# FFN groups of two blocks: side pieces handed out beside the first down products instead of the last up block's

## The chip, the cores and the metric

The kernel runs on one core of one Trainium2 chip. The metric is the device time of one launch, in microseconds. The engines are TensorE (PE in the profile, with its weight loads as PEld), VectorE (DVE), ScalarE (ACT), GpSimd (POOL) and SyncE (SP), which here only issues DMAs.

## What is computed

One inference step of a hybrid decoder layer (DEPTH 1) over 1024 prompt tokens and 64 sample tokens (8 sequences of 8), 1088 in all, model width 1024, FFN width 2752:

```
h = x + 1/2 * postnorm(SwiGLU_1(prenorm(x)))
u = prenorm(h); z = u @ w_in            # forgetting attention (8 heads x 64) and gated linear attention (4 heads)
h = h + postnorm(concat(A_out, B_out) @ w_out)
y = h + 1/2 * postnorm(SwiGLU_2(prenorm(h)))

def swiglu(x, w_gu, w_down):
    gate, up = jnp.split(x @ w_gu, 2, axis=-1)
    return (jax.nn.silu(gate) * up) @ w_down
```

All norms are RMS norms. Everything is float32; the kernel gets float32 accuracy from TensorE by splitting each operand into a high and a low part and adding three products (high x high, high x low, low x high).

## The kernel before

**Layout.** Activations lie transposed: the model width on 128 partitions in 8 slices, tokens along the free dimension. The tokens are worked in two parts, 0 to 511 (one chunk of 512 columns) and 512 to 1087 (chunks of 256 and 320 columns). Each FFN runs once for each part, so there are four passes: `f1a` and `f1b` for FFN 1, `f2` and `f3` for FFN 2.

**Blocks and groups.** The hidden width is cut into 22 blocks, block 0 being a half-wide tail. Blocks are worked in groups of two or four. For an ordinary group each block has a gate job (`job_gate`, line 674) and an up job (`job_up`, line 683): 8 slices of the model width times three products for each chunk, accumulated in one PSUM bank. The up block's evacuation (`up`, line 567) multiplies gate and up on DVE (line 539 or 540), casts the high part on ACT and subtracts it on DVE (both recorded at line 213, in `split`). When all blocks of the group are through, four down jobs (`job_down`, line 783) add the group's part of the output, two output slices at a time; within each, the products of all blocks but the last come first (`downs`, line 607), and DVE adds the result to `y` (line 646) and so frees the bank. Many groups take another path (`job_first`, `job_seven`, `job_last`) that computes gate and up in a different way; they do not go through `job_up`.

**Where two-block groups go through `job_up`.** `GROUPS` ends in [18, 19] and [20, 21], `GROUPS1` in [20, 21]. By the plans at lines 2034, 2168 and 2174 this is so in five places: block 21 in `f1a`; blocks 19 and 21 in `f1b`; blocks 19 and 21 in `f2`.

**Side pieces.** Norms, evacuations of the projection and the preparation of other stages are written as generators. `beside` (line 266) puts one into a list, `quick` or `side`. Each group of products ends in `tick(us)` (line 243) with an estimate of its own time, operations x columns x `COL` (line 44). `tick` first writes out pending evacuations (`flush`), moves the planned time `now` on, and calls `step_side` (line 253), which advances every generator of `quick` and the first of `side` whose due time has come by one piece. A piece yields the planned time until its next one; without a number that is `STEP`, 2 us. After that `tick` hands out pieces of the background list `bg` at a rate of their own.

**The norm** (line 381) is the generator that matters around the change. Its pieces are: squares and their sum (`square`, line 321; ACT, DVE, POOL) with the product `ncol` on PE that sums over partitions (line 346) and a power on POOL; a diagonal (line 366); the product `nrows` that spreads the factor over rows (line 373) with the first two slices of the scaling (line 414 with the residual added at 415, or line 439 with the splitting at 441 and 442); then two slices each. A norm with `post` and `pre` does all of this twice, with 6 planned us in between (`DREDUCE`). `need(key)` (line 376) hands out pieces without regard to their due time until the norm named is through. Around the places in question:

- before [18, 19] of `f1b`, `next2` (line 2028) puts up two norms of 256 tokens each for part one; the projection's first job needs both (line 2071);
- before [20, 21] of `f2`, the output projection puts up norms of 256 and 320 tokens for part two; the first job of `f3` needs them (line 2180).

**Order on an engine.** What is written out is given its order on each engine by the program that builds the kernel, which may place an instruction ahead of earlier ones that wait. Two things hold it: `keep_in_program_order`, and the pin in `step_side` (line 258), which puts a piece's instructions behind the last noted one of their engine while `pin` is set. `next1` (line 2014) clears it and `later_norm` (line 487) sets it.

Of the kernel before, what the change touches and what calls it, by code (L numbers as in the profile page):

```python
# [71 lines left out]
class Sums:  # L72


    def __init__(self, gate, up, f, first=None):
        self.gate, self.up, self.f = gate, up, f
        self.i = 0 if first is None else first.count
        self.first = first or self
        self.first.count = self.i + 1
# [98 lines left out]
class Step:  # L178
    def __init__(self, ctx, tc, A, O):
        self.ctx, self.tc, self.nc, self.A, self.O = ctx, tc, tc.nc, A, O  # L180
        nc = self.nc
        self.const = ctx.enter_context(tc.tile_pool(name="const", bufs=1))
        self.dram = ctx.enter_context(tc.tile_pool(name="dram", bufs=1, space=DRAM))
        self.n = 0
        self.side, self.quick, self.bg, self.pend = [], [], [], []
        self.ncw, self.ssb, self.xb = NCW, 3, 2
        self.ready = set()
        self.kept, self.later = False, []
        self.last, self.pin = {}, True
        self.calm, self.haste = False, 0.0  # L190
        self.plain, self.begin = None, lambda feed: None
        self.ups = 0
        self.held = False
        self.rate = self.due = self.now = 0.0
        self.near = None
        self.banks = dict(col=("col", 1), col2=("col", 1), rows=("rows", 1))
        cp = self.const
        self.ident = cp.tile([P, P], F32, name="ident")
        make_identity(nc, self.ident)
        self.ones = cp.tile([P, P], F32, name="ones")  # L200
        nc.vector.memset(self.ones, 1.0)
        self.mhalf = cp.tile([P, 4], F32, name="mhalf")
        nc.vector.memset(self.mhalf, -0.5)
        self.gain = cp.tile([P, 6, KB], F32, name="gain")
# [38 lines left out]
    def tick(self, us):  # L243

        self.flush()
        self.now += us
        self.step_side()
        self.due += us * self.rate
        while self.due >= 1:
            self.due -= 1  # L250
            self.piece()
# [265 lines left out]
    def ffn(self, w_gu, w_dn, f):  # L517
# [4 lines left out]
        gu = lambda i: [w_gu[i]]  # L522
# [14 lines left out]
        def times(out, t, u):  # L537
            if f.tanh:
                return nc.vector.scalar_tensor_tensor(out=out, in0=t, scalar=0.5, in1=u, op0=ALU.mult, op1=ALU.mult)
            return nc.vector.tensor_tensor(out=out, in0=u, in1=t, op=ALU.mult)  # L540

        def rooted(out, src, rb):
            self.mark = self.note(nc.vector.tensor_tensor(out=out, in0=src, in1=rb, op=ALU.mult)).ins

        def rows(o):
            return None if f.rb is None else f.rb[:, o]

        def release(c0, n, fn):

            held = [] if f.rb is None else [f.hold[c] for c in f.hold if c0 <= c < c0 + n and f.hold[c] is not None]  # L550
            held[-1].append(fn) if held else self.soon(fn)
# [15 lines left out]
        def up(hb, w, c0, n):  # L567
            o = slice(c0 - f.b0, c0 - f.b0 + n)
            ps = self.gemm(w, c0, n)
            hh, hl = hid[hb]  # L570
            t, rb = sgs[hb][:, o], rows(o)

            def evac():
                self.mark = self.note(times(t, t, ps)).ins
                if rb is not None:
                    rooted(t, t, rb)
                    self.ups += 1
                self.split(hh[:, o], hl[:, o], t, True)
            release(c0, n, evac)
# [80 lines left out]
        def job_first(g, ws):  # L660
            make(g)
            for hb in g:
                sg(hb)
            for i, (c0, n) in enumerate(f.firsts):
                f.first(i)
                if f.room and len(g) == 2 and i == len(f.firsts) - 1 and not f.early:
                    self.beside(sevens(), True)
                tail(ws[0], c0, n)
                if i == len(f.firsts) - 1:
                    self.feed.free(1, NW)  # L670
                gate(g[1], ws[1], c0, n)
                up(g[1], ws[2], c0, n)

        def job_gate(g, hb, w, chunks):
            if hb == g[0]:
                make(g)
            if f.room and hb == 2 and HB_TAIL in g and f.rb is None:
                self.beside(sevens(), True)
            sg(hb)
            for c in chunks:  # L680
                gate(hb, w, *c)

        def job_up(hb, w, chunks):
            for c in chunks:
                up(hb, w, *c)

        def seven(z, w, half, b, done):

            hi, lo = w
            xh, xl = f.operands[b]  # L690
            n = f.n // 2
            z.turn = (z.turn + 1) % 2
            ps = self.mm(n) if z.turn or self.nmm > 3 else self.other(n)
            for k in range(KB // 2):
                s = slice((half * KB // 2 + k) * P, (half * KB // 2 + k + 1) * P)
                ops = [(hi[:, s], xh[:, k]), (hi[:, s], xl[:, k]), (lo[:, s], xh[:, k])]
                for j, (a, x) in enumerate(ops):
                    nc.tensor.matmul(ps, a, x, start=(k == 0 and j == 0), stop=(k == KB // 2 - 1 and j == len(ops) - 1))  # L698
                self.tick(len(ops) * n * COL)

            def evac():
                late = self.later[:1]
                del self.later[:1]
                done(ps)
                for fn in late:
                    fn()
            self.soon(evac)
# [104 lines left out]
        jobs = []  # L812
        for g, chunks, kind in f.plan:
            if kind == "jobs":
                jobs += chunks
                continue
            if kind == "first":
                jobs.append(([gu(0), gu(1), gu(2)], lambda *ws, g=g: job_first(g, ws), 1))
                for hb in g[2:]:
                    jobs.append(([gu(2 * hb - 1)], lambda w, g=g, hb=hb, c=chunks: job_gate(g, hb, w, c), 0))  # L820
                    jobs.append(([gu(2 * hb)], lambda w, hb=hb, c=chunks: job_up(hb, w, c), 0))
            elif kind == "last":
                up4 = [gu(2 * hb - 1 + i) for hb in g for i in range(2)]
                dn = [[w_dn[d2][:, 2 * P * g[0]:2 * P * (g[-1] + 1)] for d2 in d] for d in ((0, 1), (2, 3))]
                reqs = up4[:3] + [(r, f.place(i)) for i, r in enumerate([up4[3]] + dn)]
                jobs.append((reqs, lambda *ws, g=g, c=chunks: job_last(g, ws, c), 0))
                continue
            elif kind == "sevens":
                for hb in g:
                    z, first = Part(), None  # L830
                    for i in range(4):
                        it = Sums(w_gu[2 * hb - 1], w_gu[2 * hb], f, first)
                        first = first or it
                        jobs.append(([it], lambda w, g=g, hb=hb, i=i, z=z: job_seven(g, hb, i, z, w), 0))
            else:
                for hb in g:
                    jobs.append(([gu(2 * hb - 1)], lambda w, g=g, hb=hb, c=chunks: job_gate(g, hb, w, c), 0))
                    jobs.append(([gu(2 * hb)], lambda w, hb=hb, c=chunks: job_up(hb, w, c), 0))
            if g[0] in f.between:
                jobs.append(([], f.between[g[0]], 0))  # L840
            fin = kind == "final"
            cs = [c for c in CH if chunks[0][0] <= c[0] < sum(chunks[-1])] if fin and not f.raw else chunks
            ds = []
            if kind == "sevens":
                ds = list(range(3 - len(cs)))
                jobs.append(([[w_dn[d2][:, 2 * P * g[0]:2 * P * (g[-1] + 1)]] for d2 in ds],
                             lambda *ws, g=g, ds=ds, cs=cs: downs(g, [(d2, w, None, *c, 0, None) for d2, w in zip(ds, ws) for c in cs], False), 0))
            for d2 in range(len(ds), 4):
                jobs.append(([[w_dn[d2][:, 2 * P * g[0]:2 * P * (g[-1] + 1)]]], lambda w, g=g, d2=d2, cs=cs, fin=fin: job_down(g, d2, w, cs, fin), 0))
# [1440 lines left out]
```

## Time and profile before

| | us |
|---|---|
| median of three runs | 2268.49 (2267.0 to 2269.81) |
| the profiled execution, its own time | 2272.61 |
| its span in the profile | 2270.7 |
| granted TensorE clock, mean | 0.997 |

Where the five places lie in the span, from the up block's last products to the end of the group's down products (us from the span's start):

| pass, group | up block | down products |
|---|---|---|
| `f1a`, [20, 21] | 352.35 to 357.8 | to 368.9 |
| `f1b`, [18, 19] | 700.5 to 707.1 | to 723.7 |
| `f1b`, [20, 21] | 743.6 to 750.3 | to 765.4 |
| `f2`, [18, 19] | 1749.5 to 1753.8 (its later part) | to 1765.1 |
| `f2`, [20, 21] | 1836.5 to 1842.0 | to 1856.0 |

How to read the rows: in a timeline a row is start, duration, engine, line of the kernel, operation, output tile and input tiles (names without their numbers), the form of the operands and a count; in brackets stands how long the engine had been idle before it and what released it. In the busy time by stages each row is a stretch of the span. In the groups of instructions, the numbers behind the bar are busy time in us, the mean of one in ns, and the idle time of the engine just before them.

### The profile page before, as it was taken

The numbers are of one execution on the slowest core, as the hardware profiler recorded it, in microseconds if no ns is written. First come the engines' busy times: TensorE is split into PE (matmuls) and PEld (weight loads), VectorE is DVE, ScalarE is ACT, GpSimd is POOL, SyncE is SP. The second block draws the span as 40 slices with busy tenths as digits, with TensorE's granted clock in tenths as the row PEclk, the third lists the DMA queues.
The fourth block names the chain that finished last, engine by engine and source line by source line (L and its number), as shares of the span: only waits on it lengthen the run. The fifth ranks groups of instructions, "written<-read, shape, count | busy, mean of one in ns | idle before, by whom it ended". The sixth has DMA issues, their size and how long they took to land.

```text
span 2270.7 us, 40551 instructions
## 1 busy us (share of the span) xinstructions
PE 2223.8 (98%) x15040; PEld 1984.0 (87%) x15040; DVE 1538.4 (68%) x2678; ACT 1029.0 (45%) x1783; POOL 624.9 (28%) x570
## 2 busy tenths in 40 slices
PE   9999999999999999999999999999999999999998
PEld 8898888999999877899898677777777989999998
DVE  7877886876777885566455333358775688678866
ACT  6544445433344465755344222236555556333432
POOL 2433331442223322011332312311100144234413
PEclk9999999999999999999999999999999999999999
DMA  5333333322234586563656899955554653324324
GB/s 185 122 105 96 98 102 126 102 82 82 93 112 126 166 263 198 176 195 119 202 172 201 297 336 328 316 161 141 165 152 134 199 176 112 99 89 140 103 80 139
DMA packets 203526, 357.25 MB, mean 157 GB/s; under 512 B 27265, under 2 KB 102594, under 8 KB 202946
## 3 DMA queue, kind: packets, MB, share of 16 engines
q1 hardware_dynamic: 187426, 316.36, 44.1%
q0 software_dynamic: 6544, 21.50, 2.7%
q10 hardware_dynamic: 9360, 16.81, 2.2%
q8 instruction: 119, 1.95, 0.4%
q14 instruction: 77, 0.63, 0.1%
HBM read 308.93 MB, written 45.65 MB: 156 GB/s over the span
## 4 chain that ended last, share of the span: by engine, by line
PE 47%; DVE 7%; issue 6%; ACT 3%; DMA 3%; POOL 1%; ACTq 0%; SPq 0%; DVEq 0%; POOLq 0%
PE mm L230 30%; PE mm L698 3%; PE mx L698 3%; DVE wl L213 2%; PE po L1463 2%; PE sp L1201 1%; PE po L1239 1%; PE tp L1447 1%; ACT wh L213 1%; PE pa L1596 1%; DMA wr<-in_wd 1%; DMA wr<-in_wout 1%; PE s L1430 1%; PE s L1429 1%; PE pS L1639 1%
## 5 line engine op out<-in xcount | busy, mean ns | idle before, releaser
L213 DVE TENSOR_TENSOR wl<-wr,wh 128x1024 fp32r<-128x1024 f32 (+1 forms) x251 | 290.1, 1158 | 170.0 <-ACT wh L213 152.0
L230 PE MATMUL mm<-ua,wh 128*128 128x512 f32 (+2 forms) x1264 | 391.9, 393 | 1.1 <-ACT ua L213 0.6
L213 ACT CAST wh<-wr 128x1024 fp32r<-128x1024 f32 (+1 forms) x251 | 245.3, 979 | 304.7 <-PE mm L230 175.3
L230 PE MATMUL mm<-ub,wh 128*128 128x256 f32 (+3 forms) x1760 | 372.4, 306 | 0.9 <-ACT st L968 0.5
L230 PE MATMUL mm<-hl,wh 128*128 128x256 f32 (+2 forms) x1006 | 330.1, 330 | 0.7 <-DVE hl L213 0.6
L230 PE MATMUL mm<-hh,wh 128*128 128x256 f32 (+2 forms) x958 | 320.1, 335 | 10.3 <-DVE y L646 6.3
L230 PE MATMUL mm<-hh,wl 128*128 128x256 f32 (+2 forms) x958 | 315.1, 329 | 2.2 <-DVE wl L213 2.2
L230 PEld LDWEIGHTS mm<-ub,wh 128*128 128x128 f32 (+1 forms) x1760 | 282.5, 189 | 10.7 <-issue 4.6
L230 PEld LDWEIGHTS mm<-ua,wh 128*128 128x128 f32 (+1 forms) x1264 | 225.6, 188 | 55.2 <-issue 14.1
L230 PE MATMUL mm<-ub,wl 128*128 128x256 f32 (+2 forms) x864 | 258.9, 300 | 1.0 <-DVE wl L213 1.0
L698 PE MATMUL mm<-ub,wh 128*128 128x288 f32 (+1 forms) x1328 | 258.3, 290 | 0.0
L230 PE MATMUL mm<-ua,wl 128*128 128x512 f32 (+1 forms) x624 | 239.5, 384 | 0.0
L646 DVE TENSOR_TENSOR y<-y,mm 128x256 f32<-128x256 f32 (+2 forms) x275 | 136.8, 524 | 113.8 <-PE mm L230 111.2
L698 PEld LDWEIGHTS mm<-ub,wh 128*128 128x128 f32 x1328 | 210.8, 189 | 0.0
L230 PEld LDWEIGHTS mm<-hh,wh 128*128 128x128 f32 x958 | 180.7, 189 | 32.2 <-issue 7.7
L230 PEld LDWEIGHTS mm<-hl,wh 128*128 128x128 f32 x1006 | 190.0, 189 | 15.0 <-DVE hl L213 2.0
L230 PEld LDWEIGHTS mm<-hh,wl 128*128 128x128 f32 x958 | 181.0, 189 | 16.5 <-DVE wl L213 3.7
L698 PE MATMUL mm<-ub,wl 128*128 128x288 f32 (+1 forms) x664 | 192.8, 290 | 0.0
L698 PE MATMUL mm<-ua,wh 128*128 128x288 f32 (+1 forms) x912 | 177.9, 290 | 0.8 <-ACT wh L213 0.8
L230 PEld LDWEIGHTS mm<-ub,wl 128*128 128x128 f32 x864 | 163.6, 189 | 2.8 <-DVE wl L213 1.4
L698 PEld LDWEIGHTS mm<-ua,wh 128*128 128x128 f32 x912 | 144.7, 189 | 1.3 <-ACT wh L213 1.0
L230 PEld LDWEIGHTS mm<-ua,wl 128*128 128x128 f32 x624 | 117.4, 188 | 25.3 <-issue 2.0
(341 smaller groups left out, 4240.1 us busy)
## 6 DMA issues: line engine op xcount, KB each, us to landing
wr<-in_wgu SPq DMA_DIRECT2D x72, 512.0 KB
wr<-in_wd SPq DMA_DIRECT2D x68, 512.0 KB
pr<-in_ck SPq DMA_DIRECT2D x112, 256.0 KB
wz<-in_wgu SPq DMA_DIRECT2D x100, 256.0 KB
wr<-in_win SPq DMA_DIRECT2D x46, 512.0 KB
pr<-in_cv ACTq DMA_DIRECT2D x64, 256.0 KB
wx<-in_wgu SPq DMA_DIRECT2D x50, 256.0 KB
wr<-in_wout SPq DMA_DIRECT2D x24, 512.0 KB
```

The source lines that it names most:

```text
L213: for ins in (self.nc.scalar.copy(hi, src), self.nc.vector.tensor_tensor(out=lo, in0=src, in1=hi.bitcast(F32), op=ALU.subtract)):
L230: ins = self.nc.tensor.matmul(*a, **kw)
L646: self.note(nc.vector.tensor_tensor(out=yk, in0=yk, in1=pds[d2, c0, e], op=ALU.add))
L698: nc.tensor.matmul(ps, a, x, start=(k == 0 and j == 0), stop=(k == KB // 2 - 1 and j == len(ops) - 1))
L1201: nc.tensor.matmul(sp[32 * a:32 * a + 32, 256 * hf:256 * hf + 256], qz[p % 2][:, a, s, :], raw[:, :, a * P:(a + 1) * P], start=False, stop ...
L1239: nc.tensor.matmul(po[r], pT[:, t, r], raw[:, :, a * P:(a + 1) * P], start=(t == 0), stop=False)
L1429: nc.tensor.matmul(sp[:, o:o + m], qa[:, qs], ka[:, o:o + m], start=True, stop=False)
L1430: nc.tensor.matmul(sp[:, o:o + m], qb[:, qs], kb[:, o:o + m], start=False, stop=not end)
L1447: nc.tensor.transpose(tp[:, k * P:(k + 1) * P], p[:, (k0 + k) * P:(k0 + k + 1) * P], self.ident)
L1463: nc.tensor.matmul(out, v[:, k, r], pT[:, k, s], start=(k == 0 or (k == 1 and not one)), stop=(k == last or (k == last - 1 and not one)))
L1596: nc.tensor.matmul(pa[:n, l - l0, :, a, :n // 2], E[:, l, a, :n], self.qd[:, l, a, :, :n // 2], start=True, stop=True)
L1639: nc.tensor.matmul(pS[:, a, :], km[:n, a, :], v[:n, a * 256:(a + 1) * 256], start=True, stop=True)
```

## The change

A flag `hush` is added. `job_up` sets it while the last block of a group of two is worked, and clears it behind the block; `tick` does not call `step_side` while it is set. The planned time goes on, so pieces that fall due in the block are handed out one after the other from the first tick behind it. Pending evacuations are still written out in each tick, and background pieces (`bg`) are still handed out. `job_up` gets the group as a further argument at both places that call it.

```diff
@@ __init__
-        self.held = False
+        self.held = self.hush = False
@@ tick
         self.now += us
-        self.step_side()
+        if not self.hush:
+            self.step_side()
         self.due += us * self.rate
@@ ffn
-        def job_up(hb, w, chunks):
+        def job_up(g, hb, w, chunks):
+            self.hush = len(g) == 2 and hb == g[1]
             for c in chunks:
                 up(hb, w, *c)
+            self.hush = False
@@ ffn, twice (kind "first" and the ordinary kind)
-                    jobs.append(([gu(2 * hb)], lambda w, hb=hb, c=chunks: job_up(hb, w, c), 0))
+                    jobs.append(([gu(2 * hb)], lambda w, g=g, hb=hb, c=chunks: job_up(g, hb, w, c), 0))
```

More of the change, by code (lines that the diff above doesn't have):

```diff
@@ L837, in ffn @@
                     jobs.append(([gu(2 * hb - 1)], lambda w, g=g, hb=hb, c=chunks: job_gate(g, hb, w, c), 0))
-                    jobs.append(([gu(2 * hb)], lambda w, hb=hb, c=chunks: job_up(hb, w, c), 0))
+                    jobs.append(([gu(2 * hb)], lambda w, g=g, hb=hb, c=chunks: job_up(g, hb, w, c), 0))
             if g[0] in f.between:
```

## The prediction

> **What bounds the kernel now.** I read first the page's head, then the busy time by stages, then the waits and the timelines of PE and DVE around the five places that the change touches.
>
> ```profile
> span 2270.7 us, 40551 instructions
> ...
> PE 2223.8 (98%) x15040; PEld 1984.0 (87%) x15040; DVE 1538.4 (68%) x2678; ACT 1029.0 (45%) x1783; POOL 624.9 (28%) x570
> ```
>
> TensorE is busy for 98% of the span. A change that leaves every product as it is can win only idle time of PE, and can lose only by making new idle time. So I cut out the blocks in question: the last up block of each two-block group that runs through `job_up` (five in all), and the down products behind it. (The columns: stretch, its length, then the busy time of PE, PEld, DVE, ACT, POOL, the granted clock, the DMA share and GB/s.)
>
> ```profile
> 352.35:357.80 5.45, 5.45 (x26) 4.51 (x25) 0.69 (x1) 1.12 (x2) 0.00 (x0) 1.00 0.17 48
> 357.80:368.90 11.10, 11.10 (x50) 8.94 (x49) 10.80 (x16) 5.79 (x8) 0.00 (x0) 1.00 0.46 150
> 700.50:707.10 6.60, 6.60 (x53) 6.60 (x51) 4.19 (x9) 2.75 (x8) 2.18 (x3) 1.00 0.41 116
> 707.10:723.70 16.60, 14.46 (x110) 14.11 (x109) 15.76 (x35) 6.79 (x14) 4.55 (x5) 1.00 0.37 125
> 743.60:750.30 6.70, 6.70 (x53) 6.70 (x53) 4.01 (x10) 2.84 (x7) 0.81 (x1) 1.00 0.16 42
> 750.30:765.40 15.10, 13.43 (x97) 12.67 (x96) 14.54 (x29) 9.48 (x21) 7.13 (x7) 1.00 0.43 146
> 1749.50:1753.80 4.30, 4.30 (x21) 3.56 (x20) 0.62 (x2) 0.23 (x1) 0.00 (x0) 1.00 0.21 61
> 1753.80:1765.10 11.30, 11.30 (x51) 8.86 (x50) 9.62 (x14) 3.74 (x5) 0.00 (x0) 1.00 0.44 140
> 1836.50:1842.00 5.50, 5.50 (x26) 4.52 (x26) 4.69 (x10) 3.02 (x7) 3.01 (x4) 1.00 0.34 122
> 1842.00:1856.00 14.00, 12.26 (x56) 9.52 (x55) 13.29 (x22) 5.16 (x8) 4.77 (x6) 1.00 0.53 178
> 1856.00:1865.10 9.10, 9.10 (x79) 9.10 (x78) 8.66 (x17) 7.07 (x14) 3.56 (x5) 1.00 0.90 321
> ```
>
> In pairs these are up and down of blocks 21 (first part of FFN 1), 19 and 21 (second part), 19 and 21 (first part of FFN 2); the last row is the start of the part after that. Two things are to be seen. PE never idles in an up block, and in the down stages it idles 2.14 us (16.60 − 14.46), 1.67 us and 1.74 us: 5.55 us, 0.24% of the span, is all that there is to win. And VectorE is 95 to 96% busy in just those three down stages, while it has 2.4 to 2.7 us free in the up blocks of the second part: the change takes pieces out of stages with room and puts them into full ones.
>
> **What the idle time is.**
>
> ```profile
> 717.65 0.42 PE L230 MATMUL mm<-hh,wh 128*128 128x320 f32 x1 [0.90 <-DVE y L646]
> 722.36 0.42 PE L230 MATMUL mm<-hh,wh 128*128 128x320 f32 x1 [1.24 <-DVE y L646]
> ...
> 761.62 0.36 PE L230 MATMUL mm<-hh,wh 128*128 128x256 f32 x1 [1.21 <-ACT wh L213]
> 765.43 0.70 PE L230 MATMUL mm<-ua,wh 128*128 128x512 f32 x2 [0.38 <-DVE y L646]
> ```
>
> In the second part PE waits for a bank that a late evacuation (L646) holds, and for a weight cast, not for the hidden block. The wait that the change fits stands in one place only, FFN 2, block 21:
>
> ```profile
> 1843.13 0.39 PE L230 MATMUL mm<-hh,wl 128*128 128x512 f32 x1
> 1845.16 0.47 PE L230 MATMUL mm<-hh,wh 128*128 128x512 f32 x1 [1.64 <-DVE sg L539]
> ```
>
> ```profile
> 1841.81 1.16 DVE L331 TENSOR_TENSOR ss<-ss,sq 128x320 f32<-128x320 f32 x1
> 1842.89 0.99 DVE L414 SCALAR_TENSOR_TENSOR y<-y,gain,nrows 128x320 f32<-128x320 f32 x2
> 1843.81 0.60 DVE L415 TENSOR_TENSOR y<-y,x 128x320 f32<-128x320 f32 x1
> 1844.33 0.68 DVE L539 SCALAR_TENSOR_TENSOR sg<-sg,mm 128x512 f32<-128x512 f32 x1
> ```
>
> L539, the up block's evacuation, could start at about 1842.4 and starts at 1844.33, behind rows of a norm.
>
> **When a piece is handed out is not when it runs.** One tick of planned time is operations × columns × 0.42 ns (lines 44, 318): 3 × 256 gives 0.323 us, 320 columns 0.403, 512 columns 0.645. The piece handed out at the first tick of gate block 18 holds eight squares (ACT), their sums (DVE, POOL) and the `ncol` products (PE):
>
> ```profile
> 680.19 0.40 PE L230 MATMUL mm<-ub,wh 128*128 128x256 f32 x2
> 680.42 0.28 PE L230 MATMUL mm<-ub,wl 128*128 128x256 f32 x1
> 680.54 0.51 PE L346 MATMUL ncol<-ones,ss 128*128 128x2 f32 x4
> ```
>
> ```profile
> 663.85 0.72 ACT L327 ACTIVATE ss<-y 128x256 f32<-128x256 f32 x2 [1.72 <-DMA y<-y0d]
> ```
>
> `ncol` stands exactly behind the three products of that tick; the squares of the same piece ran 16.7 us earlier. The pin of line 258 is off here (`next1` clears it at line 2014, `later_norm` sets it again much later), so ACT and DVE work goes wherever its inputs allow, and a piece's PE products keep their place far better; of those looked at, one moved, an `ncol` by 15 products:
>
> ```profile
> 1848.43 0.72 PE L346 MATMUL ncol<-ones,ss 128*128 128x2 f32 x6
> ```
>
> (planned for 53.54, eleven ticks or 33 products into the down stage; it ran behind 18). So the change moves mostly `ncol` and `nrows`, and what hangs on them.
>
> **The change part by part.**
>
> *Block 21, first part of FFN 1, and block 19, FFN 2: 0.* DVE works 0.69 of 5.45 us and 0.62 of 4.30 us there, on a weight split and evacuations: no norm is in flight, PE idles in neither down stage. A gain has nothing to come from, a loss nothing to move.
>
> ```profile
> 708.54 0.60 PE L373 MATMUL nrows<-dg,ones 128*128 128x128 f32 x4
> ...
> 747.19 0.60 PE L373 MATMUL nrows<-dg,ones 128*128 128x128 f32 x4
> ...
> 757.04 0.28 PE L230 MATMUL mm<-hh,wh 128*128 128x256 f32 x1
> ```
>
> *Block 19, second part: 0.* Two norms of 256 tokens run one after the other, with waits of 2, 4, 2, 2, 2, 6, 1, 4, 2, 2, 2 us between pieces. Counted in ticks from gate 18, before: the second `ncol` of the first norm at 19.03 (up 19), `nrows` at 24.51, the last tick of the first down part; the trace has it there (708.54). After: `ncol` at the first down tick (23.55), `nrows` at 29.03, the norm's end at 35.48 instead of 31.13. Its rows then meet the later half of a down stage that is as full as its first half. The two waits for L646 (2.14 us) go, stay or double; nothing tells which, so 0, from −2.1 to +2.1.
>
> *Block 21, second part: +1.5 us.* The second norm starts 4.3 us later, so that its 6 us wait (48.06 to 54.06) ends inside the quiet block (52.26 to 58.06), and its pieces come in the down stage: `ncol` 58.38, `nrows` 63.87, the last tick of the fourth down part, rows 4 and 5 at 68.06. The down products end at 69.68, the last rows would be due at 70.06, so `need` in `hook2` (line 2071) forces them before the first projection.
>
> ```profile
> L439 DVE SCALAR_TENSOR_TENSOR y<-y,gain,nrows 128x256 f32<-128x256 f32 x8 | 3.5, 472 | 0.0
> L442 DVE TENSOR_TENSOR ua<-y,ua 128x256 fp32r<-128x256 f32 x4 | 1.8, 453 | 0.0
> ...
> L646 DVE TENSOR_TENSOR y<-y,mm 128x256 f32<-128x256 f32 x4 | 1.6, 408 | 0.0
> ```
>
> ```profile
> L213 DVE TENSOR_TENSOR wl<-wr,wh 128x1024 fp32r<-128x1024 f32 (+1 forms) x251 | 290.1, 1158 | 170.0 <-ACT wh L213 152.0
> ```
>
> So `nrows` goes from 747.19 to 757.04, 9.85 us later. Behind it 5.3 us of DVE work (3.5 + 1.8) must be done before the projection has read its eighth slice, at 765.43 + 7 × 0.68 = 770.2 (eight such ticks took 5.45 us in the first row of the stages). From 757.4 on DVE also has about six evacuations (0.41 each, somewhat more with 320 columns: 2.7), two weight splits (1.2 each) and some square sums: 757.4 + 5.3 + 2.7 + 2.4 + 2 to 3 = 770 to 771, and delayed evacuations hold banks as at 722.36. That is 0 to 1 us for the rows and as much for the banks: 1.5, from 0 (all covered) to 5.3 (the rows run with nothing beside them).
>
> *Block 21, FFN 2: −0.5 us.* Rows 2 to 5 of the 320-token norm are no longer handed out in the up block. But rows 6 and 7 (the two L414 at 1842.89) were handed out behind L539 before the change too (planned 47.09 against up's end at 46.45), and ran ahead of it. The rest can do the same. Between 0 and the stage's whole idle time, −1.74; I take −0.5, near the row that shows the overtaking.
>
> *The start of the next part: +1.5 us.* The same norm's `ncol` moves from planned 53.54 to 58.38, its `nrows` from the first tick of the next part (57.09) to the 16th (61.93), five us in the trace:
>
> ```profile
> 1856.29 0.83 PE L373 MATMUL nrows<-dg,ones 128*128 128x128 f32 x6
> ...
> 1865.14 0.46 PE L230 MATMUL mm<-ub,wh 128*128 128x320 f32 x2
> 1865.43 0.31 PE L230 MATMUL mm<-ub,wl 128*128 128x320 f32 x1
> 1865.58 0.46 PE L230 MATMUL mm<-ub,wh 128*128 128x320 f32 x2
> ```
>
> ```profile
> 1864.92 0.88 POOL L442 TENSOR_TENSOR ub<-y,ub 128x320 fp32r<-128x320 f32 x1 [0.29 <-ACT ub L441]
> ```
>
> The 320-token products begin at 1865.14 and read a slice each 0.44 us (1865.58 − 1865.14), slice 7 at 1865.14 + 7 × 0.44 = 1868.2; the last operand is ready at 1865.8: 2.4 us to spare. After: 15 more ticks of 0.35 (680.54 − 680.19) put `nrows` 5.3 us later and the operand at 1871.1, less the 2 us of a weight split and evacuations that DVE gets done meanwhile: a stall of 0.9 to 2.9. I take 1.5, from 0 to 5.3.
>
> DMAs of moved pieces (norm inputs, the `h` stores) shift by the same 4 to 5 us in SP's queue; the loads behind them fetch weights for a later job, and the products in between hide them: 0; without that cover, a stall like the 1.21 us at 761.62.
>
> **Sum:** 0 + 0 + 0 + 1.5 − 0.5 + 1.5 = +2.5 us, on the profiled execution's own 2272.61 us. The median of the three runs is 2268.49, 0.18% lower; on that footing 2271.0 us. A measurement of this kernel tells about 0.2%, 4.5 us, from no change.
>
> **The rivals.**
>
> *It works as its words say: faster.* Evacuations come at once, the 1.64 us wait and the L646 waits go, the norms have room: −1.74 − 2.14 = −3.9, 2264.6 us. For it speaks the row at 1845.16; against it the overtaking rows and DVE's 96%. Faster by over 0.2% needs the third stage's 1.67 as well.
>
> *Nothing moves that matters.* The `ncol` and `nrows` products go back into PE gaps, and the order is the old one: 2268.5. For it: squares 16.7 us early. Against: both `nrows` above stand at their ticks.
>
> *The norms become what ends last: slower.* One mechanism: `nrows` late, then 5.3 us of DVE rows with PE waiting, at the projection and in the next part. It decides when the rows have not passed slice 7 by 770.2 and 1868.2. Price up to 5.3 + 5.3 − 0.5 = 10.1, 2278.6 us; half of that on each is +5. For it: DVE full at 750 to 765 and 1856 to 1865 (8.66 of 9.10). The Trainium skill's page "SBUF — State Buffer", section "Who interferes with whom", says that a DVE operation with two SBUF inputs and a GpSimd operation that reads SBUF block each other for a whole instruction. By that rule, estimated, the four POOL adds of the moved rows would add some 3 us to DVE's stage; the 1.16 us of L331 above, beside POOL work, agrees. The page "TensorE: Matmul & The Clock Gate", section "What's actually happening", lets the clock fall to half after an idle window of about 3.4 us; by it a full 5 us stall would cost more still. No stretch here shows it: the granted clock is 1.00 in all rows.
>
> **How the numbers follow.** Forecast 0.44, nothing moves 0.14, works 0.19, late norms 0.23. Faster by over 0.2% takes somewhat under half of the "works" case: 0.08. Slower by over 0.2% is the late norms and a tail of the forecast: 0.25. The rest, 0.67, lies within. The range runs from the "works" time, 2264.6, to just short of the full late norms, 2278.0.
>
> **What would show it.** `nrows` near 713, 757 and 1862; DVE rows L439 behind them and PE waits at the first projection and the 320-token tail; the wait for L539 still there. Wrong if `nrows` stays at its old place, if L539 starts within 0.3 us of its products' end, or if the waits for L646 vanish.

## The result, and the profile after

| | before | after |
|---|---|---|
| median of four runs, us | 2268.24 (2267.0 to 2269.81) | 2281.17 (2280.3 to 2284.51) |
| the profiled execution, its own time | 2272.61 | 2280.3 |
| its span in the profile | 2270.7 | 2278.5 |
| granted TensorE clock, mean | 0.997 | 0.994 |

The ratio of the times is 1.0055 (95%: 1.0043 to 1.0067): the change makes the kernel 12.5 us slower (9.8 to 15.2), above the range that was forecast. From here on a change in us is (ratio − 1) times 2270, with its interval.

The head of the page of after, to be read against the same two lines of before:

```profile
span 2278.5 us, 40552 instructions
...
PE 2228.8 (98%) x15040; PEld 1988.9 (87%) x15040; DVE 1536.9 (67%) x2678; ACT 1030.4 (45%) x1783; POOL 627.4 (28%) x570
```

The number of products is the same; the span is 7.8 us longer and PE counts 5.0 us more as busy: part of the time isn't idle, the products themselves took longer. The busy time by stages of after shows where (stretch, its length, busy time of PE, PEld, DVE, ACT, POOL, granted clock, DMA share, GB/s). The first three rows are the down stages of the prediction, cut somewhat wider (block 21's last up products of FFN 2 end at 1844 here), the next two the start of the part behind them, the last two the places where the time was lost:

```profile
706.60:722.90 16.30, 15.35 (x118) 15.26 (x117) 13.85 (x29) 5.39 (x10) 3.51 (x3) 1.00 0.38 132
749.20:767.30 18.10, 15.13 (x109) 14.40 (x108) 16.84 (x35) 10.63 (x24) 7.55 (x8) 1.00 0.44 146
1842.00:1858.50 16.50, 14.94 (x71) 11.87 (x70) 15.19 (x26) 6.03 (x10) 6.67 (x7) 1.00 0.51 172
1858.50:1864.30 5.80, 5.80 (x51) 5.80 (x51) 2.25 (x4) 3.51 (x6) 0.00 (x0) 1.00 1.04 400
1864.30:1878.00 13.70, 13.67 (x97) 13.15 (x95) 13.65 (x18) 7.10 (x15) 10.09 (x8) 1.00 0.64 201
832.00:846.00 14.00, 9.06 (x34) 7.16 (x35) 8.12 (x16) 3.97 (x5) 4.37 (x3) 0.88 0.63 198
1876.00:1893.00 17.00, 13.49 (x66) 11.96 (x65) 13.55 (x21) 11.28 (x25) 1.63 (x1) 0.70 0.42 127
```

The same view of before, for the start of the next part and the two places of the loss:

```profile
1858.50:1864.30 5.80, 5.80 (x51) 5.80 (x50) 5.74 (x14) 4.82 (x11) 2.69 (x3) 1.00 1.01 373
832.00:846.00 14.00, 12.35 (x60) 10.02 (x59) 11.39 (x17) 7.35 (x12) 6.08 (x5) 1.00 0.82 281
1876.00:1893.00 17.00, 15.03 (x106) 14.14 (x106) 12.54 (x18) 14.70 (x35) 3.40 (x3) 1.00 0.36 101
```

In the 14 us from 832 PE gets through 34 instructions instead of 60, in the 17 us from 1876 through 66 instead of 106, with a granted clock of 0.88 and 0.70 where it was 1.00. Neither stretch is an up block or a down stage of the change. In the down stages PE idles 0.95, 2.97 and 1.56 us, 5.48 in all, where it idled 5.55 before: the 1.2 us won behind block 19 are given back behind block 21 of the second part (2.97 for 1.67), and the sum of these stages is the old one.

PE in after, its waits and the norms' products around these places (start, duration, engine, line, operation, output and inputs, count; in brackets the idle time before it and what ended it; lines behind 247 stand one further than in before, those behind 685 three):

```profile
714.24 0.60 PE L374 MATMUL nrows<-dg,ones 128*128 128x128 f32 x4
...
755.53 0.60 PE L374 MATMUL nrows<-dg,ones 128*128 128x128 f32 x4
...
760.54 0.39 PE L230 MATMUL mm<-hh,wh 128*128 128x256 f32 x1 [0.86 <-DVE y L647]
764.88 0.41 PE L230 MATMUL mm<-hh,wh 128*128 128x320 f32 x1 [2.11 <-DVE y L647]
...
798.22 0.60 PE L374 MATMUL nrows<-dg,ones 128*128 128x128 f32 x4
...
832.74 0.50 PE L230 MATMUL mm<-wl,ua 128*128 128x512 f32 x1 [0.81 <-DVE wl L213]
...
838.85 0.89 PE L347 MATMUL ncol<-ones,ss 128*128 128x2 f32 x6 [4.21 <-DVE ss L332]
...
1845.67 0.47 PE L230 MATMUL mm<-hh,wh 128*128 128x512 f32 x1 [0.15 <-DVE sg L540]
1848.00 0.98 PE L230 MATMUL mm<-hh,wh 128*128 128x512 f32 x3 [1.41 <-ACT hh L213]
...
1850.22 0.72 PE L347 MATMUL ncol<-ones,ss 128*128 128x2 f32 x6
...
1863.48 0.83 PE L374 MATMUL nrows<-dg,ones 128*128 128x128 f32 x6
...
1878.94 0.36 PE L230 MATMUL mm<-hh,wt 128*128 128x256 f32 x1 [0.74 <-DVE sg L541]
1880.28 0.38 PE L230 MATMUL mm<-hh,wt 128*128 128x256 f32 x1 [0.87 <-ACT sg L536]
1883.82 0.64 PE L230 MATMUL mm<-hh,wt 128*128 128x320 f32 x1 [1.67 <-DVE sg L541]
```

And PE in before at the two places of the loss:

```profile
803.78 0.60 PE L373 MATMUL nrows<-dg,ones 128*128 128x128 f32 x4
...
839.40 0.83 PE L346 MATMUL ncol<-ones,ss 128*128 128x2 f32 x6 [1.65 <-DVE ss L331]
...
1878.00 0.41 PE L230 MATMUL mm<-hh,wt 128*128 128x320 f32 x1 [0.96 <-DVE sg L540]
1878.92 0.41 PE L230 MATMUL mm<-hh,wh 128*128 128x320 f32 x1 [0.36 <-ACT hh L213]
...
1881.73 0.39 PE L230 MATMUL mm<-hh,wt 128*128 128x256 f32 x1 [0.65 <-ACT y L644]
```

The three `nrows` came where they were forecast (714.24, 755.53, 1863.48 for 713, 757, 1862). The loss hangs on products far behind them. **First place:** an `ncol` of a norm for part two, in the middle of the projection, makes PE wait 4.21 us instead of 1.65. **Second place:** the first products on a new hidden block in the next part wait 3.51 us (0.74 + 0.87 + 1.67, and 0.23 at 1885.97) instead of 1.97 (0.96 + 0.36 + 0.65), and run at a clock of half from about 1880.5 to 1890.7.

How much each place costs in this pair of traces can be read by taking the same product in both. PE of after is 1.2 us behind at `z<-st,wa` (803.44 for 802.22) and 6.3 behind at `s<-ka,qa` (871.46 for 865.21): 5.0 us around the first place. It is 1.8 behind at the last `hh,wh` of block 21's down stage (1857.04 for 1855.25) and 7.9 at the first `mx` (1892.95 for 1885.09): 6.1 us around the second. Between the two it makes up 4.5 us against this execution of before, which has stretches at half clock of its own there (0.50 in 966 to 968 and in 1525 to 1530).

What VectorE did there in after:

```profile
830.26 0.49 DVE L416 TENSOR_TENSOR y<-y,x 128x320 f32<-128x320 f32 x1 [1.21 <-DMA x<-in_xT]
...
838.30 0.49 DVE L332 TENSOR_TENSOR ss<-ss,sq 128x320 f32<-128x320 f32 x1
...
1864.35 1.47 DVE L440 SCALAR_TENSOR_TENSOR y<-y,gain,nrows 128x320 f32<-128x320 f32 x3 [1.83 <-PE nrows L374]
...
1872.95 1.84 DVE L777 TENSOR_TENSOR y<-y 128x576 f32<-128x576 f32 x1
...
1878.30 0.49 DVE L541 TENSOR_TENSOR sg<-mm,sg 64x320 f32<-64x320 f32 x1
...
1883.28 0.49 DVE L541 TENSOR_TENSOR sg<-mm,sg 128x320 f32<-128x320 f32 x1
```

and in before:

```profile
838.85 0.49 DVE L331 TENSOR_TENSOR ss<-ss,sq 128x320 f32<-128x320 f32 x1
...
1865.68 0.75 DVE L774 TENSOR_TENSOR y<-y 128x576 f32<-128x576 f32 x1
...
1877.46 0.49 DVE L540 TENSOR_TENSOR sg<-mm,sg 128x320 f32<-128x320 f32 x1
```

At the first place the sum that `ncol` reads ends at the old time, 838.8 in after as 839.3 in before; what moved is `ncol` itself. In the order of the built program it and the norm products around it stand 24 to 27 products earlier on TensorE than before; the traces agree for the `nrows` shown (798.22 for 803.78, 5.6 us). At the second place VectorE first idles: in the 5.8 us from 1858.5 it works 2.25 us instead of 5.74, since `nrows` isn't there yet (1.83 us at once at 1864.35). From then on it is hardly ever free until 1886 (13.65 of the next 13.70 us), and the evacuation L541 of the 320-token up block, which stands in its queue behind the norm's rows and the preparations L777, comes at 1883.28 instead of 1877.46. Some 1.8 us of that are older (the same `ncol` of block 21's down stage runs at 1850.22 instead of 1848.43); the rest, 4.0, is about what VectorE idled, 5.74 − 2.25 = 3.5 (3.2 if before is read 1.8 us earlier, where it works 5.48 us).

### The profile page after: what moved, and what is told of

The parts are those of the page before. It is cut to its first block, busy times and chain, and to the rows that moved or that the text cites. A ratio compares the mean times of both kernels' runs of the same rounds, so it can differ in the third digit from the quotient of the medians.

```text
span 2278.5 us, 40552 instructions
## 1 busy us (share of the span) xinstructions
PE 2228.8 (98%) x15040; PEld 1988.9 (87%) x15040; DVE 1536.9 (67%) x2678; ACT 1030.4 (45%) x1783; POOL 627.4 (28%) x570
## 3 DMA queue, kind: packets, MB, share of 16 engines
q8 instruction: 120, 1.97, 0.4%
## 4 chain that ended last, share of the span: by engine, by line
PE 48%; DVE 8%; issue 5%; ACT 3%; DMA 3%; POOL 1%; ACTq 0%; SPq 0%; DVEq 0%; POOLq 0%
PE mm L230 31%; DVE wl L213 3%; PE mm L701 3%; PE mx L701 2%; PE po L1466 2%; PE tp L1450 1%; PE sp L1204 1%; PE po L1242 1%; PE pa L1599 1%; ACT wh L213 1%; DMA wr<-in_wd 1%; PE s L1433 1%; PE s L1432 1%; DMA wr<-in_wout 1%; PE pS L1642 1%
## 5 line engine op out<-in xcount | busy, mean ns | idle before, releaser
L647 DVE TENSOR_TENSOR y<-y,mm 128x256 f32<-128x256 f32 (+2 forms) x275 | 137.3, 526 | 109.4 <-PE mm L230 109.1
```

Source lines behind the costliest of these rows:

```text
L647: self.note(nc.vector.tensor_tensor(out=yk, in0=yk, in1=pds[d2, c0, e], op=ALU.add))
```

## The experiments

Theory after this reading: two causes, one at each place. (1) With both blocks of [18, 19] and [20, 21] held, the second norm of `f1b` isn't through when the projection begins. `need` in `hook2` then forces pieces, and a forced `step_side` advances every generator, the next norms' too; their products stand early from there on. (2) In FFN 2 the late `nrows` leaves VectorE idle, and what it then lacks in time comes out at the next evacuations. Rival A: the crowded down stages themselves. Rival B: all of it from one pass.

**Which pass, which block.** In `job_up` of the changed kernel, one condition each:

```diff
-            self.hush = len(g) == 2 and hb == g[1]
+            self.hush = len(g) == 2 and hb == g[1] and f.b0 == HALF                  # e1
+            self.hush = len(g) == 2 and hb == g[1] and f.tanh                        # e2
+            self.hush = len(g) == 2 and hb == g[1] and f.b0 == HALF and hb == 19     # e3
+            self.hush = len(g) == 2 and hb == g[1] and f.b0 == HALF and hb == 21     # e4
```

> Held pieces only in the second part of FFN 1 (blocks 19 and 21). Theory: the loss there is not in the down stages but in the projection behind them. Both held blocks together leave the second norm unfinished when the projection begins; the forced hand-out there also advances the next norms, whose ncol and nrows products then stand 24 to 27 products earlier on TensorE than before (their order in the built program shows -27 to -24), while their inputs come at the old time. Expected +6 us against before (about +1.7 by the projection's start, +4 to +5 at one ncol near 838 us of the span, with the granted clock at half behind it), and nothing at 1878 us. Rival A, the crowded down stages are the loss: +6 as well, but the time is lost between 707 and 766 us. Rival B, everything comes from FFN 2: 0 to +2.

> Held pieces only in FFN 2 (blocks 19 and 21 of its first part). The only change of order among the norms' products on TensorE is one nrows, 45 products later. Theory: +5 to +7 us against before, lost at 1876 to 1893 us of the span (late evacuations of the first down products, then a granted clock of half), and nothing won at the wait for L540. Rival B (all loss is in FFN 2): +12. Rival A (all in FFN 1): -1 to +1.

> Held pieces only in block 19 of the second part of FFN 1. The built order moves the norms' products 24 to 36 later in the group and the next one, and none behind 2326: the norm ends in time and nothing is forced. Theory: -1.5 to +1.5 us, no stall of over 2 us near 838 us. Rival A (crowded down stage): +3 us, half of what both blocks cost.

> Held pieces only in block 21 of the second part of FFN 1. The built order moves one nrows 21 products later, nothing else on TensorE. Theory: 0 to +1.5 us (rows somewhat late at the projection), no stall of over 2 us near 838 us: both blocks must be held together for the forced hand-out. Rival A (crowded down stage): +3 us.

| | median, us | ratio to before (95%) | change, us |
|---|---|---|---|
| e1, both blocks of `f1b` | 2276.48 | 1.0024 (1.0015 to 1.0033) | +5.4 |
| e2, FFN 2 | 2277.03 | 1.0028 (1.0015 to 1.004) | +6.4 |
| e3, `f1b` block 19 | 2271.31 | 1.0002 (0.9993 to 1.0011) | +0.5 |
| e4, `f1b` block 21 | 2274.1 | 1.001 (1.0001 to 1.0019) | +2.3 |

The before beside them had a median of 2270.77 (28 runs). e1 and e2 add up to 11.8 of the 12.5: both passes lose, about half each, and rival B falls. e3 and e4 add up to 2.8 of e1's 5.4. They were expected at no more than 1.5 each; e4 is above that, and its interval holds anything from 0.2 to 4.3, so rival A isn't excluded by these four alone. One expectation missed: e3 and e4 do wait over 2 us near 840, 2.21 and 2.18, and e2, whose order there is that of before, 2.27. So that wait varies from one trace to the next. In all the runs whose order there is nearly that of before it lies between 1.22 (e11) and 2.27 (e2), with the 1.65 of before in the middle; e1 has the 4.21 of after:

```profile
839.65 1.12 PE L347 MATMUL ncol<-ones,ss 128*128 128x2 f32 x6 [4.21 <-DVE ss L332]
```

**Taking each cause away.** e5 is e1 with a forced hand-out that moves the needed norm alone; e7 is e2 with the wait ahead of the norm's second half shortened, so that `nrows` is back at its place. (The edits are shown shortened, here and below.)

```diff
# e5, in hook2
-                self.need(("p", CH[1][0]))
+                while ("p", CH[1][0]) not in self.ready:
+                    quick, self.quick = self.quick, []
+                    self.step_side(True)
+                    self.quick = quick + self.quick
# e7, in norm
-            yield DREDUCE
+            late = key == "f2" and c0 == CH[3][0]
+            yield 1.16 if late else DREDUCE
```

**Putting each cause into the kernel before**, with nothing held: e6 forces one extra step, e8 lengthens the wait behind that norm's second diagonal.

```diff
# e6, in hook2 of before
                 self.need(("p", CH[1][0]))
+                self.step_side(True)
# e8, in norm of before
-            yield rest
+            yield 6.84 if key == "f2" and c0 == CH[3][0] else rest
```

> As e1 (held pieces in both blocks of the second part of FFN 1), but the forced hand-out at the projection's start advances only the norm that is needed, and leaves the other generators at their due times. The built order then has the later norms' ncol and nrows products at the places of before (0 to 3 products away), instead of 24 to 27 earlier; the down stages are as in e1. Theory (forced hand-out): +0 to +2.5 us against before, and no PE wait of 4 us near 838 us. Rival A (crowded down stages): +5.5 us as in e1.

> The kernel before, nothing held, with one extra forced hand-out at the projection's start: every generator gets one piece ahead of its time. The built order has the later norms' ncol and nrows products 27 to 30 earlier, as in e1, and no other change of order in the down stages. Theory: +3 to +5.5 us against before, with a PE wait of about 4 us for an ncol near 838 us and the granted clock at half behind it. Rival A (crowded down stages): -1 to +1 us.

> As e2 (held pieces in FFN 2), with the 320-token norm's wait between its two halves cut from 6 to 1.16 planned us, so that its second nrows stands where it stood before. Built order: TensorE, ScalarE, GpSimd and SyncE as before, and of VectorE only a few rows around L539 of block 21 stand otherwise. Theory (the late nrows is the loss): -1 to +1 us against before; the wait of some 1.6 us at the first products on the hidden block stays. Rival (the down stage of block 21 is the loss): +4 to +6 us.

> The kernel before, nothing held, with the wait ahead of that norm's second nrows lengthened by 4.84 planned us: nrows stands 45 products later, as in e2. Built order: that of e2 on every engine, but for the few VectorE rows around L539. Theory (VectorE idles until the late nrows, is then behind by that much, and the evacuations of the next part come late by it): +5 to +7 us against before, lost between 1876 and 1893 us, with PE waits of 2 us and more for L540 and a granted clock of half. Rival: 0 to +1.5 us.

| | median, us | ratio to before (95%) | change, us |
|---|---|---|---|
| e5, held, needed norm forced alone | 2267.62 | 0.9986 (0.9977 to 0.9995) | −3.2 |
| e6, not held, all forced | 2274.57 | 1.0015 (1.0005 to 1.0024) | +3.4 |
| e7, held, `nrows` in time | 2269.61 | 0.9993 (0.9983 to 1.0002) | −1.6 |
| e8, not held, `nrows` late | 2277.53 | 1.0028 (1.0018 to 1.0037) | +6.4 |

The before beside them: 2270.96 (35 runs); one of e6's twelve runs took 5555 us, and its ratio leaves it out. e5 holds exactly what e1 holds and has lost all of e1's +5.4, though its down stages wait for L647 as long as those of after (3.9 us in both); its `nrows` is back at 804.46 and its `ncol` waits 1.28 us. e8 holds nothing and has all of e2's +6.4. Rival A falls. e5 and e7 came out below what was expected (0 to +2.5, −1 to +1), and the two sizes of the first cause don't meet: taking it away changes e1 by 8.6 us, putting it into before by 3.4 (1.1 to 5.5). That it costs is shown; how much, only roughly. PE in e6 at the first place:

```profile
833.29 0.58 PE L230 MATMUL mm<-wl,ua 128*128 128x512 f32 x1 [2.36 <-DVE wl L213]
...
836.14 1.44 PE L346 MATMUL ncol<-ones,ss 128*128 128x2 f32 x6 [0.98 <-DVE ss L331]
```

One thing here isn't as expected: not one wait of 4 us for `ncol` but 2.36 us for a weight's low part, which on VectorE has come behind the early norm's rows, and 0.98 for `ncol`. The sum, 3.34, and the clock (the `ncol` group takes 1.44 us, 0.83 in before) are of the size expected. PE in e8 at the second place shows the wait of after almost to the digit (1.72 for 1.67; 2 us and more were expected):

```profile
1880.53 0.64 PE L230 MATMUL mm<-hh,wt 128*128 128x320 f32 x1 [1.72 <-DVE sg L541]
```

**Both causes by hand.** The kernel before, nothing held, with the lines of e6 and e8 together:

> The kernel before, nothing held anywhere, with the two suspected causes put in by hand together: the extra forced hand-out at the projection's start (e6) and the late second nrows in FFN 2 (e8). Theory (these two are the whole loss): +9.8 us against before, the sum of e6 and e8 (3.4 + 6.4), 7.5 to 13, as the changed kernel's +12.7. If holding the pieces costs something of its own in the up blocks or down stages, this stays well below the changed kernel, at +7 or less.

Its median is 2285.69 us, beside a before of 2273.0 (9 runs): ratio 1.0054 (1.0041 to 1.0068), +12.3 us, against 1.0055 for the change. The stages of e12, at the two places (the second one shifted by what was lost ahead of it):

```profile
832.00:846.00 14.00, 11.47 (x34) 8.89 (x35) 6.62 (x14) 2.94 (x4) 1.38 (x2) 0.63 0.57 186
1884.00:1901.00 17.00, 13.05 (x69) 10.95 (x69) 14.41 (x21) 12.49 (x29) 0.78 (x1) 0.80 0.42 124
```

34 instructions, as in after (with less idle time and a lower clock, 0.63 for 0.88), and 69 for 66. Holding the pieces in the up blocks costs nothing that can be seen beside these two.

**Both repairs, and two further steps.** e9 is the whole change with the lines of e5 and e7. e10 adds a later `ncol` at the first place, where even before PE waits 1.65 us; e11 pins the pieces behind block 21's evacuation in FFN 2, so that L540 really comes first; the pin stays on through the down stage and holds each piece behind the down evacuations written out ahead of it, too.

```diff
# e10, in norm, in place of e7's line
+            late = (key, c0)
+            yield {("f2", CH[3][0]): 1.16, ("p", CH[3][0]): 8.6}.get(late, DREDUCE)
# e11, e9 and at the end of job_up; start5 clears it
+            if f.tanh and hb == 21:
+                self.pin = True
```

> The whole change (pieces held in all five blocks) with both repairs: the forced hand-out at the projection advances only the norm that is needed (e5), and the wait in the 320-token norm of FFN 2 is cut from 6 to 1.16 planned us (e7). Theory: what the change loses hangs on these two places alone, so this is not slower than before; the sum of e5 and e7 is -3.3 - 1.4 = -4.7, expected -5 to 0 us against before and -17 to -11 against the changed kernel. Rival (a further loss in the crowded down stages): +2 us or more.

> e9, and the second ncol of the 320-token norm in the projection (where PE waits 1.5 to 2.3 us near 839 us in all kernels whose order there is that of before) handed out 2.6 planned us later, 12 products in the built order. If a late hand-out of ncol is what takes the wait away: 1.5 to 2.5 us better than e9, no wait over 0.5 us there and a granted clock of 1.00 behind it. If the wait comes from something else, or moves to the nrows behind it: the same as e9 within 1 us.

> e9, and in FFN 2 the pieces handed out behind block 21 are pinned behind its evacuation, so that L540 really comes first on VectorE, as the change's words say. In the built order the norm's ncol then stands 31 and its nrows 18 products later. If the prompt evacuation is a gain by itself: the wait of 1.6 us for L540 near 1843 us goes, -1.6 us against e9. Theory: it goes, but VectorE idles later until nrows and the evacuations of the next part come late by some 18 of the 45 products of e8, +2 us; together 0 to +2 us against e9.

| | median, us | ratio to before (95%) | change, us |
|---|---|---|---|
| e9, change with both repairs | 2272.54 | 0.9996 (0.9987 to 1.0005) | −0.9 |
| e10, e9 with a later `ncol` | 2271.1 | 0.9988 (0.9979 to 0.9997) | −2.7 |
| e11, e9 with the evacuation first | 2277.42 | 1.0023 (1.0013 to 1.0032) | +5.2 |

(Before beside them: 2273.11, 27 runs.) e9 takes back the whole loss. It was expected near the sum of e5 and e7, −4.8; at −0.9 (−3.0 to +1.1) it is well short of that, and the three intervals are too wide to say whether the two gains don't add up or were never so large. In e10 the wait is gone; its `ncol` stands without idle time before it, and the clock is full behind it:

```profile
842.47 0.72 PE L347 MATMUL ncol<-ones,ss 128*128 128x2 f32 x6
...
840.00:843.00 3.00, 3.00 (x18) 2.55 (x16) 2.87 (x4) 1.50 (x3) 0.00 (x0) 1.00 0.84 234
```

That is 1.8 us better than e9 in the middle, as expected, but within what the two intervals leave open. e10 and e5 are the two versions whose interval lies below before, by 0.1% in the middle; which of them is better, these runs don't say.

e11 is the rival "it works as its words say" carried out. PE in e11:

```profile
1849.58 0.50 PE L230 MATMUL mm<-hh,wh 128*128 128x512 f32 x1 [1.85 <-DVE y L648]
1854.31 0.50 PE L230 MATMUL mm<-hh,wh 128*128 128x512 f32 x1 [1.70 <-DVE y L648]
...
1881.53 0.41 PE L230 MATMUL mm<-hh,wt 128*128 128x320 f32 x1 [2.91 <-DVE sg L542]
```

The wait for L540 is gone. In its place PE waits 3.55 us in the same down stage for banks (L648, the evacuation of the down products, behind the norm's rows), and the late `nrows` costs 2.91 us in the next part: 4.9 us worse than e9 by the medians, more than the 0 to 2 expected. In this stage, in which VectorE is full, the order that is good for one of its customers is bad for the next.

## Why the prediction was wrong

The sign of its sum was right, +2.5, and the forecast of no measurable change was wrong: 12.5 us slower. By its own steps:

- **Block 21 of the first part of FFN 1, block 19 of FFN 2, 0:** right as far as the runs go; e12 has the whole loss without them.
- **Block 19, second part, 0:** e3 measures +0.5 (−1.6 to +2.5). Of the two waits for L646 one is left (0.95 in after): right.
- **Block 21, second part, +1.5:** e4 measures +2.3 (0.2 to 4.3); in after the wait stands where it was forecast, as late evacuations that hold banks (2.11 us at 764.88; 2.10 and 0.93 in e4). Right in size, by one half of its mechanism: for the rows themselves PE doesn't wait at the projection's start.
- **The step that failed is in the same paragraph:** "the last rows would be due at 70.06, so `need` in `hook2` (line 2071) forces them before the first projection". I read what the forced step does to the norm that is needed, and stopped. The same call advances every generator in `quick`, here the next two norms' statistics, and with them all their later products, by 24 to 27 products. No term of the sum stood for it. e6 prices it alone at +3.4 (1.1 to 5.5).
- **Block 21, FFN 2, −0.5:** 0. Rows did run ahead of L540 again, but fewer: it starts 0.7 us behind its products' end (1844.84 for 1844.16) where it was 2.2 (1844.33 for 1842.16), and the wait for it falls from 1.64 to 0.15 us. Nothing is won, since PE then waits 1.41 us for the cast `hh`, which on ACT stands behind squares of the norm (1847.35): 1.56 us in all. In e11, where the evacuation does come first, the kernel is slower (+5.2).
- **The second step that failed, the start of the next part, +1.5 (0 to 5.3):** `nrows` was right (1863.48 for 1862), the price and where it is paid were not: +6.4 (4.1 to 8.4) in e8. I asked whether the last operand would reach the 320-token tail in time, and it does: from 1864.3 to 1878.0 PE is busy 13.67 of 13.70 us. But I gave VectorE "the 2 us of a weight split and evacuations" as a credit and forgot the rest of its queue. In before it works 27.8 of the 29.3 us from 1856.7 to 1886, more than PE with 27.3. What it idles for a late `nrows` it has not made up when it comes to the last thing that it must do before PE can go on, the evacuation some 20 us later (1863.48 to 1883.28).
- **The clock:** "No stretch here shows it" was true of the stretches shown, at 1.00 in all rows, but not of the trace of before: there PE runs at 0.50 from 1525 to 1530, behind waits of 0.81 and 0.68 us, and from 966 to 968, behind a wait of 1.52 (at 964.50). What I made of it was wrong: I left half clock out of the price of a stall of 1 to 2 us. In after it is 0.70 for the 17 us from 1876.
- **The late norms as a rival, up to +10.1:** the nearest in size, and by the wrong way: neither the first projection nor the tail waited 5 us for rows.

The range ended at 2278.0. It took the two known stalls as the worst case and left no room for what a moved piece sets off further on.

Two things stay open: why e5 is 3.2 us better than before, and with it the exact price of the forced hand-out. That would take more than one trace of each. That the sums of the early `ncol` keep their old time because the norm's input comes late (1.21 us for the DMA at 830.26) is read from the trace and wasn't tried.

## What to carry to other kernels

Ask of a helper that is called late "until X is ready" what else it moves: one forced hand-out put all later norms of its stage out of step. Follow a delayed piece not to its own consumer but through the queue of the engine that is full: it is paid at the last instruction in that queue for which the bound engine waits. A wait on a nearly full engine is only worth removing if the order that removes it doesn't put another customer behind. And where one trace of each version can differ by luck elsewhere, compare them product by product around the place in question.

## What the hardware showed that was not expected

**A short wait can cost more than its length, in some executions.** The same wait of 1.64 us for the same evacuation stands in the traces of before (1845.16, shown ahead) and e8:

```profile
1842.14 0.47 PE L230 MATMUL mm<-hh,wh 128*128 128x512 f32 x1 [1.64 <-DVE sg L540]
...
1842.20:1846.20 4.00, 3.89 (x10) 2.83 (x11) 2.95 (x6) 0.98 (x3) 0.00 (x0) 0.62 0.76 259
```

and the 4 us behind it in before:

```profile
1845.20:1849.20 4.00, 3.90 (x19) 2.90 (x20) 3.89 (x8) 1.57 (x3) 0.00 (x0) 1.00 0.77 265
```

Ten instructions in place of nineteen. The Trainium skill's page "TensorE: Matmul & The Clock Gate", section "What's actually happening", has the clock fall to half after an idle window of about 3.4 us, and lets that window run freely, not from the start of the kernel. That it is a matter of chance where in the window a wait falls agrees with these two rows; that the window must be idle as a whole does not, at 1.64 us. At the second place after runs at half clock from about 1880.5 (a product of 256 columns takes 0.28 us at 1879.13 and 0.42 at 1880.66), behind waits of 0.74 and 0.87 us; the 1.67 us come while it does. Before has waits of 0.96 and 0.36 there and keeps its full clock. This may be a part of why executions of one kernel spread here by several us (before: 2266.08 to 2278.22 in 35 runs, with a mean granted clock of 0.999 in the shortest and 0.994 in the longest), and why the spans of two single profiles don't size a loss.

**VectorE beside GpSimd.** The rows L774 and L777 above are the same operation, 0.75 us at 1865.68 and 1.84 at 1872.95. The first had GpSimd beside it for its first 0.1 us only, the second all the time:

```profile
1872.70 1.47 POOL L94 TENSOR_TENSOR y<-wx,y 128x512 f32<-128x512 f32 x1
1874.13 1.81 POOL L94 TENSOR_TENSOR wx<-y,wx 128x512 f32<-128x512 f32 x1
```

That agrees with the Trainium skill's page "SBUF — State Buffer", section "Who interferes with whom", by which a VectorE instruction with two SBUF inputs contends with a GpSimd instruction that reads SBUF. Before has such rows as well (1.83 us at 1872.82): summed over 1861 to 1879, an estimate from the rows, they are longer than alone by some 4 us in before and 5 in after. So it isn't what sets the two kernels apart; it may be part of why VectorE can't make up what it lost. The prediction's estimate of some 3 us for the four GpSimd operations of the moved rows isn't borne out: beside them, at 1866.59 and 1869.45, the operation L443 takes 0.71 us instead of 0.48.
